# A diffusion trunk on one core: where layer 1's S5 and Hyena preparations stand beside layer 0's context mixer

## The chip, the cores and the metric

The kernel runs on one core of a Trainium2 chip. The time is what the device takes for one execution, in microseconds (us). Engines: PE (TensorE, matrix products; it has two clock levels, 1.2 and 2.4 GHz, and the profile gives the share it was granted), DVE (VectorE), ACT (ScalarE), POOL (GpSimd, which here mainly issues gathers and a few loads), and SP, whose queue issues most DMAs.

## The reference

Two layers work on 512 latent tokens (`x`) and 256 context tokens (`xc`) of width 1024. The context leaves after layer 0.

```python
for layer in range(DEPTH):                       # DEPTH = 2
    h  = modulate(rms_norm(x, norm1_g), sh1, sc1)
    hc = modulate(rms_norm(xc, norm1_g), mc[0], mc[1])
    y, yc = token_mixer(h, hc, ...)              # attention, Hyena, S5, gates, merge
    x = x + g1 * y
    h = modulate(rms_norm(x, norm2_g), sh2, sc2)
    x = x + g2 * peer_ffn(h, wq, keys, u, v)
    if need_ctx:                                 # layer 0
        xc = xc + mc[2] * yc
        hc = modulate(rms_norm(xc, norm2_g), mc[3], mc[4])
        xc = xc + mc[5] * peer_ffn(hc, wq, keys, u, v)

def peer_ffn(x):                                 # per block of 128 tokens
    s = einsum('bthsk,hsnk->bthsn', (x @ wq), sub_keys)    # scores, 8 heads x 2 halves
    s_top, i_top = top_k(s, 16)                            # picks
    best, pos = top_k(all sums of two halves, 16)
    gate = softmax(best)
    act = gelu(x . u[expert]);  return sum(gate * act * v[expert])
```

The Hyena branch needs the spectrum of a filter that depends on the layer's weights alone, and the S5 branch needs tables of powers, also from weights alone. Those two are the preparations of the title.

## The kernel before

One Python program writes all instructions; nothing loops on the chip. `weave` takes several generators, each with a lane and a price per step, and always steps the one whose priced time is least, so it fixes the order in which the engines' queues are filled. Between two steps a generator yields a cost in a planner's unit. A scheduler may still shift single instructions.

After layer 0's latent mixer one `weave` runs five chains:

- the main chain: `ctx_rest`, the context's mixer (norm, queries, attention, `hyena_in`, `hyena_out`, `s5_out`, merge), whose end is marked `c1`; then `ctx_side`, the context's norm, scores and picks for its feed-forward part;
- `peer_u`: 128 u blocks, each a load `w` of 128 experts' rows, a split in two parts (`wh` on ACT, `wl` on DVE), 24 matmuls of 512 columns into `pu`, a gelu `ua`, a store;
- `aside`, the side chain that the change touches;
- `gather`: for the two context blocks, 128 gathers of expert rows `gx` by POOL, each with a product on DVE (L1196), then 128 gathers with a weighted add (L170); `gx` has four buffers. It starts when the context's picks and the `gx` pool are there;
- layer 1's modulation vectors.

A latent block is scored (`scores`, PE), picked (`pick`: top-16 searches on DVE, no PE work), and made into a table (`table`, 32 steps: one `ohB` and four `ohA` operations on DVE, four matmuls, a copy `ge`; every fourth step a store of 1 MB). When the side chain has all four tables and u is done, `peer_v` runs 128 v blocks of 24 matmuls into `pa`, with the rest of the gathers beside it. Then layer 1 begins.

`s5_prep` (L368) is a long chain of small DVE operations, then `X<-cmp,cmq` operations of 128x512, transposes on PE, copies on ACT and stores on SP. `hy_prep` (L610) makes a filter, splits it (`FH`, `FL`), and for each half of the columns multiplies it by four DFT matrices; each is a 1 MB load `dft` that POOL issues (L676), in one buffer for layer 1.

Of the kernel before, what the change touches and what calls it, by code (L numbers as in the profile page):

```python
# [23 lines left out]
TL = 512  # L24
# [22 lines left out]
class Trunk:  # L47
# [52 lines left out]
    def weave(self, *chains):  # L100


        run = [[0.0, i, g, w, lane] for i, (g, w, lane) in enumerate(chains)]
        outer, held = self.lane, []
        while run:
            assert len(held) < len(run), (self.done, [c[1] for c in run])
            c = min(x for x in run if x not in held)
            self.lane = c[4]
            known = len(self.done)
            try:  # L110
                d = next(c[2])
            except StopIteration:
                run.remove(c)
                held = []
                continue
            if d == WAIT:
                held = held * (len(self.done) == known) + [c]
                continue
            for x in held:
                x[0] = max(x[0], c[0])  # L120
            held = []
            c[0] += (2.6 if d is None else d) * (c[3]() if callable(c[3]) else c[3])
        self.lane = outer
# [4 lines left out]
    def until(self, *ks):  # L128
        while any(k not in self.done for k in ks):
            yield WAIT  # L130
# [5 lines left out]
    def part(self, g, k):  # L136

        for d in g:
            if d == k:
                return  # L140
            yield d
# [9 lines left out]
    def mark(self, k):  # L151
        self.done.add(k)
        yield 0.0
# [90 lines left out]
    def rows(self, pool, l, j, i, tag="rowb", bufs=1):  # L244
        b = self.t(pool, [128, D], tag=tag, bufs=bufs)
        self.nc.sync.dma_start(b, self.mod[l][j:j + 1, i * D:(i + 1) * D].to_broadcast([128, D]))
        return b
# [1170 lines left out]
    def run(self):  # L1418
# [21 lines left out]
        def mods(l, groups, *vecs):  # L1440
            for g in groups:
                yield from self.mod_group(l, g)
            for w in vecs:
                vec[l, w] = self.mod_vec(l, 3 * w, w)

        def chain(*gens):
            for g in gens:
                yield from g
# [8 lines left out]
        call, until, mark, weave, part = self.call, self.until, self.mark, self.weave, self.part  # L1457


        x1, x2, c1, c2 = new(xl), new(xl), new(xc), new(xc)  # L1460
# [12 lines left out]
        sc, scC = rows(4), rows(2)  # L1473
        act = [self.d([128, TL]) for _ in range(128)]
        C = {}
        hs = []

        def aside():
            yield from self.norm_to(hs[0], x1, vec[0, 1], 0, True)
            self.done.add("h")  # L1480
            yield from self.s5_prep(1, self.S[1], True)
            yield from self.hy_prep(1, TL, self.K[1, TL], True)
            self.done |= {("hy", 1), ("room", 1)}
            with self.pool("pg", True) as pg, ExitStack() as ex:
                hn, w, dot = ([self.t(pg, [128, n]) for _ in range(2)] for n in (D, 3 * 128, 128))
                ids = [self.t(pg, [128, 128], I32) for _ in range(2)]
                pc = [x.rearrange("p (a h k) -> p a h k", a=3, h=8) for x in w]
                C.update({q: (hn[q], pc[q], ids[q], dot[q]) for q in range(2)})
                self.done.add("pg")
                pk = [self.t(pg, [128, 3, 8, 16]) for _ in range(2)]  # L1490
                yield from self.scores(0, hs[0], sc)
                for q in range(5):
                    if q < 4:
                        yield from self.pick(0, sc[q], pk[q % 2])
                    if q:
                        yield from self.table(pk[(q - 1) % 2], G[q - 1])
                    if q == 4 and "gx" not in C:
                        yield from until("c1")
                    if "c1" in self.done and "gx" not in C:
                        C["gx"] = ex.enter_context(self.pool("gx", True))  # L1500
                        self.done.add("gx")
                self.done.add("tabs")
                yield from self.stop("tables")
                yield from until("c2")

        def ctx_side():
            yield from until("pg")
            hn = [C[q][0] for q in range(2)]
            with self.pool("ph") as ph:
                hA = self.halves(ph, TC)  # L1510
                yield from self.norm_to(hA, c1, vec[0, 1], 1, False, hn)
                self.natural(ph, 0, 1, hn)
                yield from self.peer_scores(0, ph, hA, TC, scC)
            for q in range(2):
                yield from self.pick(0, scC[q], C[q][1], C[q][2], False)
                self.done.add(("ids", q))

        def gather():
# [3 lines left out]
            self.done.add("c2")  # L1522

        side, gather = aside(), gather()
        with self.pool("ha") as ha:
            hs.append(self.halves(ha, TL))
            with self.psum(m=4, u=2, s=2), self.pool("ua") as ua:
                weave((chain(self.ctx_rest(0, xc, c1, vec[0, 0], st[0]), mark("c1"), ctx_side()), lambda: 1.1 if "c1" in self.done else 1.0, "m"),
                      (chain(until("h"), self.peer_u(0, ua, hs[0], TL, lambda i: act[i], "tabs"), mark("u")), lambda: 1.2 if "c1" in self.done else 10.0, "u"),
                      (part(side, "tables"), lambda: 1.25 if "c1" in self.done else 1.23 if "pg" in self.done else 0.8, "s"),  # L1530
                      (self.while_(gather, "tabs"), 1.69, "s"), (mods(1, range(6), 0, 1), 1.26, "m"))
            self.done.add(("mods", 1))
            with self.pool("pv", True) as pv:
                vl = self.peer_v(0, pv, hs[0], lambda i: act[i], G, x1, self.store(x2), 0)
                next(vl)
                with self.psum(a=7, x=1):
                    weave((vl, 1.0, "m"), (gather, 1.5, "s"))
# [12 lines left out]
        act = [self.d([128, 128 * nd]) for _ in range(128)]  # L1550
        sc = rows(4)
# [14 lines left out]
        with self.pool("pg", True) as pg, self.pool("fin") as fin:  # L1566
# [7 lines left out]
            with self.pool("ha") as ha:  # L1574
                h = self.halves(ha, TL)
# [141 lines left out]
```

## Time and profile before

| | |
|---|---|
| median of 3 runs | 5657.81 us (5644.19 to 5683.04) |
| profiled execution | 5662.23 us, span 5660.2 us |
| PE, DVE, ACT, POOL busy | 87%, 66%, 31%, 25% of the span |
| mean granted PE clock | 0.925 |
| DMA | 1333 MB, 236 GB/s on average |

Busy is the time in which an engine has an instruction in work. Ends of matmuls are modelled, and they overlap, so a PE that reads as busy may still have room. The granted clock is a share of 2.4 GHz.

### The profile page before, as it was taken

What the parts mean: (1) busy time and instruction counts of PE and PEld (TensorE: products, weight loads), DVE (VectorE), ACT (ScalarE), POOL (GpSimd) and SP (SyncE); (2) the same over time, 40 slices, a digit from 0 to 9 for tenths busy, and PEclk for the clock granted to TensorE, in tenths of its full rate; (3) what the DMA queues carried; (4) which work ended last, traced back from release to release, by engine and by line L of the source; (5) the groups of instructions that cost most, each with busy time, mean ns of one, the idle gap of its engine ahead of it and who ended that gap; (6) DMA issues with size and microseconds to landing.
All of it is one profiled execution on the core that took longest, in us unless ns stands there. A gap on an engine that the chain in (4) does not pass through costs nothing.

```text
span 5660.2 us, 72445 instructions
## 1 busy us (share of the span) xinstructions
PE 4899.3 (87%) x25801; PEld 4022.5 (71%) x25801; DVE 3729.2 (66%) x7594; ACT 1758.3 (31%) x2651; POOL 1426.1 (25%) x1626
## 2 busy tenths in 40 slices
PE   6798978869997888998888887998889588899898
PEld 5676657648885777786666676875678587798687
DVE  5643436644499899987676775534435989788755
ACT  3222423314432322332222223333233133333233
POOL 0003500000002343433444440405000322254400
PEclk7899989889998999999998998998999899999999
DMA  6557335666556888899999986561545777799975
GB/s 207 190 185 263 106 117 183 201 205 185 176 179 207 306 291 314 319 325 343 319 317 311 320 307 205 166 224 58 157 157 168 242 252 243 256 338 333 333 239 176
DMA packets 641793, 1333.38 MB, mean 236 GB/s; under 512 B 56437, under 2 KB 342390, under 8 KB 626328
## 3 DMA queue, kind: packets, MB, share of 16 engines
q1 hardware_dynamic: 522776, 871.53, 47.1%
q0 software_dynamic: 118656, 457.23, 23.0%
q8 instruction: 203, 3.33, 0.2%
q14 instruction: 158, 1.29, 0.1%
HBM read 1147.01 MB, written 181.49 MB: 235 GB/s over the span
## 4 chain that ended last, share of the span: by engine, by line
PE 27%; DVE 12%; DMA 11%; issue 10%; POOL 4%; ACT 1%; SPq 1%; POOLq 0%; DVEq 0%; ACTq 0%
PE pa L181 9%; PE two L181 4%; PE ps L181 4%; PE pu L181 3%; POOL gx L1183 3%; PE px L181 2%; DMA va<-t 2%; PE pf L181 2%; DMA gx<-in_peer_v_dram,t 2%; DVE t L170 2%; DVE wl L160 2%; PE pm L181 2%; DMA gx<-in_peer_un_dram,t 1%; DVE gx L1196 1%; DMA t<-ge 1%
## 5 line engine op out<-in xcount | busy, mean ns | idle before, releaser
L176 ACT CAST wh<-w 128x1024 fp32r<-128x1024 f32 (+1 forms) x550 | 545.9, 993 | 1611.2 <-PE pu L181 395.3
L160 DVE TENSOR_TENSOR wl<-w,wh 128x1024 fp32r<-128x1024 f32 (+1 forms) x550 | 639.4, 1164 | 555.4 <-ACT wh L176 545.3
L1183 POOL DMA_INDIRECT gx<-in_peer_un_dram,t x384 | 527.9, 1375 | 1501.1 <-DVE t L1196 691.6
L181 PE MATMUL pa<-xl,vwh 128*128 128x512 f32 x1664 | 673.1, 405 | 124.1 <-DVE xl L160 123.7
L1183 POOL DMA_INDIRECT gx<-in_peer_v_dram,t x384 | 543.6, 1416 | 680.1 <-DVE t L170 579.9
L181 PE MATMUL pa<-xh,vwh 128*128 128x512 f32 x1664 | 665.8, 401 | 28.1 <-ACT xh L176 21.4
L181 PE MATMUL pu<-t,wh 128*128 128x512 f32 x2048 | 659.0, 403 | 28.5 <-ACT ua L173 20.7
L181 PE MATMUL pa<-xh,vwl 128*128 128x512 f32 x1664 | 665.1, 400 | 1.2 <-DVE ss L167 1.1
L181 PE MATMUL pm<-t,wh 128*128 128x384 f32 (+1 forms) x2432 | 586.0, 328 | 59.1 <-ACT wh L176 54.4
L170 DVE SCALAR_TENSOR_TENSOR t<-gx,t,t 128x1024 f32<-128x1024 f32 x381 | 488.4, 1282 | 35.2 <-DMA gx<-in_peer_v_dram,t 33.3
L1196 DVE CUSTOM_DVE_ANT_0 gx<-gx,t 128x1024 f32<-128x1024 f32 x384 | 465.3, 1220 | 57.8 <-DMA gx<-in_peer_un_dram,t 57.4
L181 PEld LDWEIGHTS pm<-t,wh 128*128 128x128 f32 x2432 | 431.1, 196 | 77.7 <-ACT wh L176 72.2
L181 PEld LDWEIGHTS pa<-xl,vwh 128*128 128x128 f32 x1664 | 323.0, 194 | 213.2 <-DVE xl L160 147.0
L181 PEld LDWEIGHTS pu<-t,wh 128*128 128x128 f32 x2048 | 389.6, 194 | 111.6 <-ACT ua L173 26.8
L181 PE MATMUL pu<-t,wl 128*128 128x512 f32 x1024 | 412.9, 404 | 60.4 <-DVE wl L160 60.4
L181 PE MATMUL pm<-t,wl 128*128 128x384 f32 (+1 forms) x1216 | 396.9, 329 | 49.1 <-DVE wl L160 49.0
L181 PEld LDWEIGHTS pa<-xh,vwh 128*128 128x128 f32 x1664 | 322.0, 194 | 103.6 <-ACT xh L176 27.7
L176 ACT CAST vwh<-gt 128x512 fp32r<-128x512 f32 (+1 forms) x256 | 145.3, 568 | 794.9 <-PE pa L181 671.2
L181 PEld LDWEIGHTS pa<-xh,vwl 128*128 128x128 f32 x1664 | 323.5, 194 | 70.8 <-DVE vwl L160 3.5
L176 ACT CAST xh<-x 128x1024 fp32r<-128x1024 f32 x256 | 268.2, 1048 | 252.4 <-DMA x<-in_peer_v_dram 208.0
L160 DVE TENSOR_TENSOR xl<-x,xh 128x1024 fp32r<-128x1024 f32 x256 | 312.7, 1221 | 26.2 <-ACT xh L176 25.8
L160 DVE TENSOR_TENSOR gt<-va,gt 128x512 f32<-128x512 f32 (+1 forms) x256 | 156.6, 622 | 262.2 <-DMA va<-t 107.9
(371 smaller groups left out, 9154.3 us busy)
## 6 DMA issues: line engine op xcount, KB each, us to landing
w<-in_peer_u_dram SPq DMA_DIRECT2D x256, 512.0 KB
x<-in_peer_v_dram SPq DMA_DIRECT2D x256, 512.0 KB
w<-in_in_w_dram SPq DMA_DIRECT2D x128, 512.0 KB
t<-ge SPq DMA_DIRECT2D x56, 1024.0 KB
gt<-t SPq DMA_DIRECT2D x112, 512.0 KB
w<-in_mod_w_dram SPq DMA_DIRECT2D x96, 512.0 KB
dft<-in_dft_dram POOLq DMA_DIRECT2D x32, 1024.0 KB, 6.8
t<-ua SPq DMA_DIRECT2D x128, 256.0 KB
```

Source lines behind the costliest of these rows:

```text
L160: return (e or self.nc.vector).tensor_tensor(out=out, in0=a, in1=b, op=op)
L170: self.nc.vector.scalar_tensor_tensor(out=out, in0=a, scalar=s, in1=b, op0=op0, op1=op1)
L176: self.nc.scalar.copy(h, x)
L181: self.nc.tensor.matmul(out, l, r, start=start, stop=stop)
L1183: self.nc.gpsimd.indirect_dma_start(out=g, out_offset=None, in_=src, in_offset=bass.IndirectOffsetOnAxis(ap=ids[:, k:k + 1], axis=0))
L1196: self.nc.vector.tensor_tensor_reduce(out=g, in0=g, in1=x, scale=1.0, scalar=0.0, op0=OP.mult, op1=OP.add, accum_out=dot[:, c:c + 1])
```

## The change

In `aside` the latents' scores move ahead of everything else. The picks and tables follow at once. `s5_prep` and `hy_prep` of layer 1 move into the loop over the blocks, to the point where `c1` is found done (it is waited for at the fourth round now, not at the fifth), after the `gx` pool is taken. The price of a u block ahead of `c1` goes from 10 to 5.

```diff
         def aside():
             yield from self.norm_to(hs[0], x1, vec[0, 1], 0, True)
             self.done.add("h")
-            yield from self.s5_prep(1, self.S[1], True)
-            yield from self.hy_prep(1, TL, self.K[1, TL], True)
-            self.done |= {("hy", 1), ("room", 1)}
+            yield from self.scores(0, hs[0], sc)
             with self.pool("pg", True) as pg, ExitStack() as ex:
...
                 pk = [self.t(pg, [128, 3, 8, 16]) for _ in range(2)]
-                yield from self.scores(0, hs[0], sc)
                 for q in range(5):
                     if q < 4:
                         yield from self.pick(0, sc[q], pk[q % 2])
                     if q:
                         yield from self.table(pk[(q - 1) % 2], G[q - 1])
-                    if q == 4 and "gx" not in C:
+                    if q == 3 and "gx" not in C:
                         yield from until("c1")
                     if "c1" in self.done and "gx" not in C:
                         C["gx"] = ex.enter_context(self.pool("gx", True))
                         self.done.add("gx")
+                        yield from self.s5_prep(1, self.S[1], True)
+                        yield from self.hy_prep(1, TL, self.K[1, TL], True)
+                        self.done |= {("hy", 1), ("room", 1)}
...
-                      (chain(until("h"), self.peer_u(...), mark("u")), lambda: 1.2 if "c1" in self.done else 10.0, "u"),
+                      (chain(until("h"), self.peer_u(...), mark("u")), lambda: 1.2 if "c1" in self.done else 5.0, "u"),
```

DVE's queue in the context's `hyena_out` (`hy`, `hz`, `hyl` are its products and split). Before, S5 operations `cmp`, `cmq`, `X` stand between them:

```order
L160 TENSOR_TENSOR cmp_9615<-X_9414,t_8211 128x512
L160 TENSOR_TENSOR cmq_9616<-X_9414,t_8235 128x512
L160 TENSOR_TENSOR X_9414<-cmp_9615,cmq_9616 128x2x16x16
L160 TENSOR_TENSOR hy_9593<-pm_9569,hk_9567 128x512
L160 TENSOR_TENSOR hz_9594<-pm_9569,hk_9567 128x512
L160 TENSOR_TENSOR hy_9593<-hy_9593 128x256
L160 TENSOR_TENSOR cmp_9669<-X_9414,t_8211 128x512
L160 TENSOR_TENSOR hy_9593<-hz_9594 128x256
L160 TENSOR_TENSOR cmq_9670<-X_9414,t_8235 128x512
```

After, at the same place of the context's mixer, a pick's searches (MAX, MAX_INDEX, MATCH_REPLACE on a block's scores `scin`):

```order
L1053 MAX_INDEX i_2034_9571<-s_2033_9570,scin_9966 128x8
L1054 MATCH_REPLACE mr_10074<-s_2033_9570,scin_9966 128x128
L1055 MAX s_2033_9570<-mr_10074 128x8
L1056 MAX_INDEX i_2034_9571<-s_2033_9570,mr_10074 128x8
L160 TENSOR_TENSOR hy_9880<-pm_9849,hk_9847 128x512
L160 TENSOR_TENSOR hz_9881<-pm_9849,hk_9847 128x512
L160 TENSOR_TENSOR hy_9880<-hy_9880 128x256
L1054 MATCH_REPLACE mr_10080<-s_2033_9570,scin_9966 128x128
L160 TENSOR_TENSOR hy_9880<-hz_9881 128x256
```

So the S5 operations left this place and a pick came.

POOL's queue at layer 1's `hy_prep`. Before, the `dft` loads stand alone or between the merge's small adds `mf`:

```order
L676 DMA dft_10408<-in_dft_dram 128x2048
L676 DMA dft_10650<-in_dft_dram 128x2048
L160 TENSOR_TENSOR mf_10585<-mf_10585,sg_10665 128x256
L676 DMA dft_10788<-in_dft_dram 128x2048
L160 TENSOR_TENSOR mf_10585<-mf_10585,sg_10734 128x256
L676 DMA dft_10928<-in_dft_dram 128x2048
```

After, they stand between the context's gathers:

```order
L1183 DMA gx_17108<-in_peer_un_dram,t_9563 128x1024
L676 DMA dft_16656<-in_dft_dram 128x2048
L1183 DMA gx_17148<-in_peer_un_dram,t_9563 128x1024
L1183 DMA gx_17166<-in_peer_un_dram,t_9563 128x1024
L1183 DMA gx_17215<-in_peer_un_dram,t_9563 128x1024
L676 DMA dft_16729<-in_dft_dram 128x2048
L1183 DMA gx_17221<-in_peer_un_dram,t_9563 128x1024
```

A load and two to five gathers now follow each other in one queue.

DVE's queue at the end of the last table, just ahead of the first v block (`gt`, `xl`). Before, `wl` of the last u blocks stands among the last steps:

```order
L160 TENSOR_TENSOR ohB_21433<-t_82,pt_20379 128x512
L167 TENSOR_SCALAR ohA_21432<-t_82,pt_20379 128x128 x4
L160 TENSOR_TENSOR wl_21514<-w_21512,wh_21513 128x1024
L160 TENSOR_TENSOR wl_21548<-w_21546,wh_21547 128x1024
L160 TENSOR_TENSOR ohB_21449<-t_82,pt_20379 128x512
L167 TENSOR_SCALAR ohA_21448<-t_82,pt_20379 128x128 x4
L160 TENSOR_TENSOR wl_21582<-w_21580,wh_21581 128x1024
L160 TENSOR_TENSOR gt_21620<-va_21634,gt_21620 128x32x16
```

After, steps and gather adds alone:

```order
L160 TENSOR_TENSOR ohB_21638<-t_82,pt_21094 128x512
L170 SCALAR_TENSOR_TENSOR t_9557<-gx_21631,t_9559,t_9557 128x1024
L167 TENSOR_SCALAR ohA_21637<-t_82,pt_21094 128x128 x4
L170 SCALAR_TENSOR_TENSOR t_9557<-gx_21634,t_9559,t_9557 128x1024
L160 TENSOR_TENSOR ohB_21654<-t_82,pt_21094 128x512
L167 TENSOR_SCALAR ohA_21653<-t_82,pt_21094 128x128 x4
L170 SCALAR_TENSOR_TENSOR t_9557<-gx_21650,t_9559,t_9557 128x1024
L170 SCALAR_TENSOR_TENSOR t_9557<-gx_21666,t_9559,t_9557 128x1024
L160 TENSOR_TENSOR gt_21686<-va_21700,gt_21686 128x32x16
```

The last `wl` moved ahead of the whole last table.

## Rows read from the trace of the kernel before

**Rows 1.** The page's span in 40 equal slices: busy tenths of two engines.

```profile
PE   6798978869997888998888887998889588899898
...
DVE  5643436644499899987676775534435989788755
```

**Rows 2.** Windows: busy us (instructions) of each engine, PE clock, DMA share, GB/s.

```profile
core 0: us, PE busy (x) PEld busy (x) DVE busy (x) ACT busy (x) POOL busy (x), PEclk, DMA share, GB/s
956.00:1186.00 230.00, 182.54 (x1168) 136.76 (x1168) 156.22 (x382) 70.63 (x131) 2.17 (x4) 0.82 0.63 202
1186.00:1340.00 154.00, 121.31 (x809) 98.31 (x808) 64.25 (x106) 50.31 (x74) 8.33 (x12) 0.90 0.70 206
1340.00:1517.00 177.00, 177.00 (x1160) 161.56 (x1160) 69.82 (x89) 74.49 (x105) 11.46 (x12) 1.00 0.56 167
1517.00:1789.00 272.00, 232.79 (x1237) 196.54 (x1237) 232.74 (x929) 95.98 (x144) 22.19 (x18) 0.94 0.60 190
1789.00:2522.00 733.00, 658.89 (x3270) 552.12 (x3269) 682.41 (x1604) 222.47 (x328) 299.05 (x217) 0.96 0.86 305
...
2547.00:3404.00 857.00, 733.83 (x3017) 588.35 (x3018) 627.92 (x784) 203.03 (x255) 374.83 (x270) 0.92 0.93 320
```

**Rows 3.** The chain that ended last, 2405 to 2425: start, us, what.

```profile
2412.93 5.46 PE pu L181 x24
```

**Rows 4.** Timeline of DVE, 2457 to 2459.5: start us, us, engine line op.

```profile
2455.89 1.22 DVE L160 TENSOR_TENSOR wl<-w,wh 128x1024 fp32r<-128x1024 f32 x1
2457.03 0.69 DVE L160 TENSOR_TENSOR ohB<-t,pt 128x512 f32<-128x512 f32 x1
2457.63 1.11 DVE L167 TENSOR_SCALAR ohA<-t,pt 128x128 f32<-128x128 f32 x4
2458.66 0.69 DVE L160 TENSOR_TENSOR ohB<-t,pt 128x512 f32<-128x512 f32 x1
```

**Rows 5.** DVE's groups, 1556 to 1789: busy us, mean ns | idle before.

```profile
L160 DVE TENSOR_TENSOR wl<-w,wh 128x1024 fp32r<-128x1024 f32 x39 | 47.3, 1213 | 4.7 <-ACT wh L176 4.7
...
L1196 DVE CUSTOM_DVE_ANT_0 gx<-gx,t 128x1024 f32<-128x1024 f32 x14 | 17.0, 1217 | 4.1 <-DMA gx<-in_peer_un_dram,t 4.1
```

**Rows 6.** DVE's groups, 956 to 1340 (`cmp` and `cmq` cost as `X` does).

```profile
L160 DVE TENSOR_TENSOR X<-cmp,cmq 128x512 f32<-128x512 f32 x32 | 21.9, 686 | 16.6 <-PE ps L181 16.3
...
L160 DVE TENSOR_TENSOR FL<-fst,FH 128x512 fp32r<-128x512 f32 x8 | 5.5, 690 | 1.7 <-ACT FH L176 1.6
...
L160 DVE TENSOR_TENSOR win<-win,ps 128x512 f32<-128x512 f32 x8 | 5.4, 684 | 2.5 <-PE ps L181 1.9 <-DMA win<-in_hy_win_dram 0.6
```

**Rows 7.** Timelines of POOL and PE, 1186 to 1330: in brackets idle before, releaser.

```profile
1229.25 0.53 POOL L676 DMA_DIRECT2D dft<-in_dft_dram  x1 [35.05 <-PE ps L181]
1242.96 0.53 POOL L676 DMA_DIRECT2D dft<-in_dft_dram  x1 [13.18 <-PE ps L181]
1266.78 0.53 POOL L676 DMA_DIRECT2D dft<-in_dft_dram  x1 [23.29 <-PE ps L181]
1276.65 0.53 POOL L676 DMA_DIRECT2D dft<-in_dft_dram  x1 [9.35 <-PE pm L181]
...
1236.67 0.58 PE L181 MATMUL ps<-FH,dft 128*128 128x256 f32 x1 [4.06 <-DMA dft<-in_dft_dram]
...
1258.53 0.58 PE L181 MATMUL ps<-FH,dft 128*128 128x256 f32 x1 [11.39 <-DMA dft<-in_dft_dram]
...
1273.21 0.39 PE L181 MATMUL ps<-FH,dft 128*128 128x256 f32 x1 [1.16 <-DMA dft<-in_dft_dram]
```

**Rows 8.** The chain that ended last, 3430 to 3460: from the v loop into layer 1.

```profile
3434.11 1.29 DVE t L170
3435.41 6.93 DMA gx<-t
...
3445.84 5.97 DMA w<-in_s_w_dram
...
3454.21 1.12 DVE junk L256
```

More of the change, by code (lines that the diff above doesn't have):

```diff
@@ L1528, in run @@
                 weave((chain(self.ctx_rest(0, xc, c1, vec[0, 0], st[0]), mark("c1"), ctx_side()), lambda: 1.1 if "c1" in self.done else 1.0, "m"),
-                      (chain(until("h"), self.peer_u(0, ua, hs[0], TL, lambda i: act[i], "tabs"), mark("u")), lambda: 1.2 if "c1" in self.done else 10.0, "u"),
+                      (chain(until("h"), self.peer_u(0, ua, hs[0], TL, lambda i: act[i], "tabs"), mark("u")), lambda: 1.2 if "c1" in self.done else 5.0, "u"),
                       (part(side, "tables"), lambda: 1.25 if "c1" in self.done else 1.23 if "pg" in self.done else 0.8, "s"),
```

## The prediction

> **What bounds the kernel now.** I read the slices of the span first [rows 1]: VectorE (DVE) is at 9 tenths from about 1,560 us to 2,510 us and at 2 to 6 tenths before that. Then I cut that part of the span into stretches and asked for each engine's busy time and TensorE's (PE's) granted clock in each [rows 2]; the page's 87% for PE mixes stretches with different limits. What the reader is to see there:
>
> - 956 to 1340 (layer 1's S5 preparation, then its Hyena preparation, beside the context's mixer): nobody is full. PE is busy 183 + 121 = 304 of 384 us, at a clock of 0.82 and 0.90, DVE 156 + 64 = 220.
> - 1340 to 1517 (the latents' scores beside the merge): PE is busy for all 177 us, clock 1.00, DVE for 70.
> - 1517 to 1789 (context scores, picks): PE and DVE 233 each, of 272.
> - 1789 to 2522 (tables, gathers, u blocks): DVE 682 of 733, 93%. PE's 659 look alike but are not: a u block of 24 matmuls takes 5.46 us where nothing holds it [rows 3], and the 96 blocks here need 524 us.
>
> So c1, the end of the context's mixer (about 1,517), divides a part that waits from a part that DVE sets.
>
> **What moves, in DVE time.** Costs are from one start to the next, since records overlap a little [rows 4]: a one-hot step of a table is 2458.66 - 2457.03 = 1.63 us, a `wl` 1.14 us, an operation of 128x512 0.60 us. A pick: DVE's 233 us in 1517 to 1789, less 47 of `wl`, 17 of products [rows 5] and some 10 of other things, are 159 for about 3.6 picks, so 44 us each. By the order of the built programs, ahead of c1 now stand the picks of latents 0 and 1 and 14 of the 32 steps of table 0, and 11 u blocks where there were 6.
>
> Out of the part behind c1 go 2 x 44 + 14 x 1.63 + 5 x 1.14 = 117 us of DVE. Into it come the S5 preparation (32 each of `X`, `cmp`, `cmq` at 0.60, 58 us [rows 6], and some 20 of small operations, an estimate), the Hyena preparation (`FL` and `win` 11 us [rows 6], and as much again in small ones, 22) and 20 more gather adds, which the order shows ahead of the last table's end (123, were 103), at about 1.2: 124 us. **DVE, the engine that sets this part, is not relieved: +7 us.** What can be won or lost is how well the waits of either part are covered.
>
> **Ahead of c1.** PE's own work stays: 192 dft matmuls of 256 columns and 192 small ones leave; at half of 5.46/24 = 0.23 us [rows 3] that is 44 us. Five u blocks (27) and the step matmuls (56, some 6) enter: -11. What the stretch 956 to 1340 holds beyond its work is 80 us of idle PE (384 - 304) and what the low clock costs, 183 x 0.18 + 121 x 0.10 = 45. The Hyena preparation's waits for its 1 MB `dft` loads go, and the scores, PE work without chains, move to where attention's chains leave gaps. But the 16 S5 outputs and `hyena_out` now run beside picks, which give PE nothing, and their DVE operations stand in line behind clumps of MAX8 rows. Nearest rows: 1340 to 1517 has no idle PE, 956 to 1186 has 20%. I let about half go, 60 us; with the 11, **-71**. Ends: everything goes, -136; nothing but PE's own work, -10.
>
> **Behind c1.** The Hyena preparation now stands among gathers and u blocks. Its `dft` tile has one buffer: POOL issues a load, it lands, PE does its 24 matmuls, POOL may issue the next. The trace has rounds of 13.7, 23.8 and 9.9 us (issues at 1229.25, 1242.96, 1266.78, the next at 1276.65), with landings of 7.4, 15.6 and 6.4 us until PE starts [rows 7]. Mean 15.8; eight rounds make 126 of the stretch of 154 us, 28 are the rest. I take the same with 6 us for u blocks in the way: 160 us. DVE's work in it by the order: 41 products (1.16), 18 `wl` and the 22 us, 90 us, at 93% 97 us. So some **+63** of the DVE-bound part in which DVE is not full. Ends: rounds of 9.9, +10; rounds of 23.8 (218 us), +121. I keep the mean, since DMA share is 0.63 to 0.70 where these rounds ran and 0.86 where they go.
>
> By the Trainium skill ("DMA: Bandwidth & Descriptors", section "Anatomy of one DMA") a load costs 2.0 us and its bytes over 436 GB/s, an estimate of 4.4 us for 1 MB. The landings in the trace, 6.4 to 15.6 us, say otherwise; by the page's price a round would be some 10 us, the term +11, and the sum some 50 us lower.
>
> POOL's queue: behind each `dft` load that waits for PE stand gathers, whose products DVE must do in order, ahead of the next `wl`. Four `gx` buffers let the gathers run three ahead, about 3 x 3.4 us (733 us for 217 gathers, POOL's count in [rows 2]), so a wait of 10 us is covered; the 13.18 us one is, but for 3. I book nothing more. SP's queue: 32 stores of `X` and the S5 weight stores now stand among u loads; a late `w` load costs up to 5.97 us [rows 8]. This, and the last table, whose 32 steps stand without any u block behind u's end (DVE stays full with steps and adds, PE has almost nothing, and its clock must rise again), I put at **+5**, ends 0 and +20. With DVE's +7: **+75**, from +17 to +148.
>
> **Behind the tables.** In 2547 to 3404 the gathers lack 20 adds, 10.5 MB, 33 us at 320 GB/s if DMA sets that stretch, nothing if not; PE is busy 734 of 857 us and the fixed pattern is its own, so **-5**. At the end, the last add now stands at 3434.11, its residual's load takes 6.93 us, and layer 1's norm only begins at 3454.21 [rows 8]. By the order the gather now ends some ten blocks of the v loop earlier, so this chain goes: **-15**, from -5 to -20.
>
> **Sum.** -71 + 75 - 5 - 15 = -16 us on the profiled execution's 5662 us, 5646. The median of the three runs is 4 us under that execution; I say **5645**.
>
> **Rivals.**
>
> *No change worth measuring (my forecast).* About 1%, 57 us, is what a measurement of this kernel can tell from no change. The stalls move with the preparations. Own range 5600 to 5700.
>
> *Faster: the regimes fill each other.* Picks take DVE where PE was the limit, preparations take PE where DVE is, and the stalls of 956 to 1340 vanish, as in 1340 to 1517, where no PE time is idle. Nearly all of it goes (-130) and the rounds are short (+10, +7, +5 behind c1): with -20 at the end -128, 5535. Half-way cases lie at 5570. For it: 220 of 384 us of DVE busy, room for both picks. Against it: DVE's sum behind c1 does not fall. The Trainium skill ("Perfetto Trace Analysis", section "Optimization Strategy") says that where the most-contended engine changes over time, interleaving the regimes may help; that is this rival, and 1517 to 1789, where both engines hold 86%, agrees with it.
>
> *Slower: POOL's queue closes a loop.* A `dft` load waits for PE; the gathers queued behind land late; DVE stands at their product, with `wl` behind it; PE's u block waits for that `wl`, and the next round's matmuls stand behind the block. Rounds then last as the longest of the trace: +121. With -40 ahead of c1, +7, +10 and -15: +83, 5745. It decides from waits of POOL at `dft` above the 10 us that three gathers cover. For it: two of the three waits shown are longer (13.18, 23.29) [rows 7]. Against: they were long when POOL had nothing else and came early.
>
> **Chances.** Forecast 0.53, faster 0.27, slower 0.20. For over 1% faster I give 0.27, within 1% 0.52, over 1% slower 0.21. The range, 5560 to 5740, leaves out the full gain and the far end of the loop.
>
> **What would show it.** The end of the context's mixer (last context `my` on DVE) at about 1,445 instead of 1,517, with PE's clock above 0.9 in between; DVE busy below 70% for some 150 us while `ps<-FH,dft` matmuls run beside gathers; the first `pa` matmul within 30 us of 2,547; a stretch of some 100 us before it with PE under a third busy; and no residual load between the last v block and layer 1. I am wrong if the context's mixer ends before 1,400 or after 1,500, if `dft` rounds are 10 or 24 us, or if the v loop's 857 us move by more than 20.

## The result, and the profile after

The changed kernel takes 5715.05 us (median of 5 runs, 5712.15 to 5720.62), the kernel before 5656.69 us in the same session. The ratio is 1.0099, with a 95% interval from 1.0075 to 1.0122: about 56 us slower, right at the 57 us that the prediction took as the least that can be told from no change. The forecast was 5645. The time lies inside the range given, but the change went the other way.

The slices of the span of the changed kernel:

```profile
PE   6898878978997889886888888999789688899898
...
DVE  5643435366778679997676775444345889788755
```

Against [rows 1], VectorE's row of nines behind the context's mixer is broken up: sixes and sevens stand there now. Windows of the kernel before, the parts ahead of and behind c1 and two stretches of the second (the columns are those of [rows 2]):

```profile
929.00:1525.00 596.00, 504.12 (x3289) 410.59 (x3290) 307.61 (x615) 215.59 (x339) 21.96 (x28) 0.89 0.63 196
1525.00:2547.00 1022.00, 905.10 (x4547) 758.81 (x4545) 912.63 (x2529) 319.74 (x475) 321.24 (x235) 0.95 0.79 274
1525.00:1585.00 60.00, 52.77 (x303) 45.29 (x302) 32.44 (x105) 28.43 (x49) 0.00 (x0) 0.94 0.60 190
1585.00:1725.00 140.00, 133.10 (x721) 112.37 (x720) 139.02 (x624) 54.97 (x79) 0.00 (x0) 1.00 0.54 166
```

The same of the changed kernel: both parts first, then stretches of them in order of time, and all that follows the tables:

```profile
933.00:1501.00 568.00, 491.45 (x3223) 398.70 (x3224) 329.18 (x883) 229.51 (x348) 16.69 (x20) 0.93 0.60 186
1501.00:2628.00 1127.00, 960.06 (x4612) 796.93 (x4610) 918.57 (x2284) 318.94 (x474) 347.48 (x264) 0.89 0.79 269
...
1218.00:1392.00 174.00, 128.09 (x813) 99.63 (x813) 123.42 (x403) 56.40 (x79) 6.39 (x6) 0.87 0.55 158
...
1521.00:1601.00 80.00, 80.00 (x524) 71.06 (x524) 44.77 (x81) 37.15 (x66) 0.00 (x0) 1.00 0.61 194
...
1599.00:1730.00 131.00, 126.80 (x651) 107.22 (x650) 111.01 (x424) 42.27 (x63) 5.19 (x4) 0.93 0.52 167
1730.00:1878.00 148.00, 110.88 (x433) 86.56 (x432) 130.86 (x359) 29.96 (x40) 41.91 (x34) 0.83 0.73 237
...
1951.00:2067.00 116.00, 98.90 (x464) 84.35 (x463) 55.63 (x89) 24.99 (x37) 35.77 (x34) 0.87 0.85 289
...
2507.00:2607.00 100.00, 61.90 (x267) 54.29 (x267) 94.75 (x196) 18.06 (x32) 40.96 (x36) 0.60 0.81 275
...
2628.00:5717.00 3089.00, 2704.29 (x13431) 2266.97 (x13431) 2055.03 (x3637) 942.13 (x1370) 894.01 (x919) 0.94 0.73 246
```

What the reader is to see. Ahead of c1 the kernel is 28 us shorter (596 to 568), behind c1 105 us longer (1022 to 1127), and from the first v block on 24 us shorter (5660 - 2547 = 3113 to 3089). The sum, +53, and a start that is 4 us later make the 57 us between the two spans. Behind c1 VectorE does the same work in both, 913 and 919 us; it is idle for 208 us where it was idle for 109. That is the loss. The view of waits says for what VectorE waits there, first in the kernel before (us in total, times, longest):

```profile
DVE wl L160 <- ACT wh L176: 24.0, 10, 4.4
```

and in the changed kernel:

```profile
DVE wl L160 <- ACT wh L176: 95.0, 24, 11.0
DVE gt L160 <- DMA va<-t: 18.4, 1, 18.4
...
DVE t L160 <- DMA wse<-t: 6.6, 1, 6.6
DVE X L160 <- PE ps L181: 6.3, 1, 6.3
DVE wse L360 <- DMA t<-wse: 5.9, 1, 5.9
```

The first row leads through ACT to PE: ACT's `wh` of a u block waits for the matmuls of an earlier one to free its buffer (315 us of ACT's waits in this part; 384 before, but then VectorE had picks to do meanwhile). So VectorE has done all that its queue holds ahead of a `wl` and stands at it, while PE is behind with the u blocks. The second row (`gt`) is no difference: the first v block's `gt` waits for 19.0 us in the kernel before as well, but starts just behind the window's end at 2547, so that the view leaves it out. Three places hold most of it. At 1521 to 1601 the context's scores, u blocks and the second half of the first table stand together; all three need PE, which has no idle time at full clock, and VectorE works for 45 of 80 us. At 1599 to 1878, in the S5 preparation, 37 us are idle. At 1878 to 2067, in the Hyena preparation, 83 are; the row from 1951 shows its dft matmuls, PE at 99 and VectorE at 56 of 116 us. In the kernel before, VectorE is idle for 28 us at 1525 to 1585, most of them beside the end of the latents' scores and the context's norm. Nearly all of the context's scores (key products from 1564 to 1662) and u blocks then stood beside picks: 140 us in which both engines are full.

### The profile page after: what moved, and what is told of

It reads as the page before. It is cut to its first block, busy times and chain, and to the rows that moved or that the text cites. A ratio compares the mean times of both kernels' runs of the same rounds, so it can differ in the third digit from the quotient of the medians.

```text
span 5717.6 us, 72447 instructions
## 1 busy us (share of the span) xinstructions
PE 4935.1 (86%) x25801; PEld 4048.4 (71%) x25801; DVE 3730.8 (65%) x7594; ACT 1771.0 (31%) x2659; POOL 1422.0 (25%) x1626
## 4 chain that ended last, share of the span: by engine, by line
PE 34%; DVE 18%; DMA 15%; issue 9%; POOL 4%; ACT 2%; SPq 1%; DVEq 0%; POOLq 0%; ACTq 0%
PE pa L181 9%; PE ps L181 6%; PE pm L181 6%; PE two L181 4%; PE pu L181 3%; DMA va<-t 3%; POOL gx L1183 3%; DVE wl L160 2%; DMA gt<-t 2%; DVE t L170 2%; PE px L181 2%; PE pf L181 2%; DVE gx L1196 2%; DMA t<-ge 2%; DMA gx<-in_peer_v_dram,t 1%
## 5 line engine op out<-in xcount | busy, mean ns | idle before, releaser
L181 PE MATMUL pu<-t,wh 128*128 128x512 f32 x2048 | 671.6, 408 | 27.8 <-ACT ua L173 24.7
L181 PE MATMUL ps<-ohB,ohA 128*128 128x128 f32 x1792 | 275.1, 307 | 76.0 <-DVE ohA L167 38.8
```

The source lines that it names most:

```text
L181: self.nc.tensor.matmul(out, l, r, start=start, stop=stop)
```

## The experiments

Differences to the kernel before are given as ratios with their 95% intervals, and as us by the ratio and 5655 us. My first theory, A, was that the preparations bring chains and waits into the part behind c1, and the rival, B, that something else does, the last table without u blocks above all; C, D and E came up on the way and are stated in the texts on record.

**One part undone at a time.** Layer 1's S5 preparation back ahead of the scores:

```diff
+            yield from self.s5_prep(1, self.S[1], True)
             yield from self.scores(0, hs[0], sc)
...
-                        yield from self.s5_prep(1, self.S[1], True)
```

> The changed kernel with layer 1's S5 preparation back ahead of the latents' scores; the Hyena preparation stays behind c1. Theory A (the loss sits behind c1, where the preparations put chains and waits into the part that VectorE sets): 58 us of VectorE's work and some 40 us of its waits leave that part, some 60 us come back ahead of c1: 5,670 to 5,690 us. Theory B (the loss is the last table without u blocks, because u ends early; the preparations cost the same at either place): 5,700 to 5,730 us.

Measured: 5699.03 us, ratio 1.0073 (1.0049 to 1.0097), +41. The Hyena preparation back:

```diff
+            yield from self.hy_prep(1, TL, self.K[1, TL], True)
             yield from self.scores(0, hs[0], sc)
...
-                        yield from self.hy_prep(1, TL, self.K[1, TL], True)
```

> The changed kernel with layer 1's Hyena preparation back ahead of the latents' scores; the S5 preparation stays behind c1. Theory A: the 154 us stretch behind c1 in which VectorE was busy for 94 goes, with it some 60 us of waits and 22 us of work, and some 50 us come ahead of c1: 5,675 to 5,695 us. Theory B: 5,700 to 5,730 us.

Measured: 5700.82, 1.0079 (1.0052 to 1.0107), +45. The u price back:

```diff
-lambda: 1.2 if "c1" in self.done else 5.0, "u"),
+lambda: 1.2 if "c1" in self.done else 10.0, "u"),
```

> The changed kernel with the u blocks' price ahead of c1 at 10, as before: by the order of the program 6 u blocks ahead of c1 instead of 11, and u ends 5 blocks later, still ahead of the last table's end. Theory A: PE's 27 us move from ahead of c1, where PE is near full, to behind it, where it has room: 5,690 to 5,715 us. Theory B: the stretch of the last table without u blocks shortens by half: 5,680 to 5,700 us. If the u blocks ahead of c1 fill gaps there: 5,715 to 5,730 us.

Measured: 5708.05, 1.0093 (1.0064 to 1.0121), +53. And the tail without u blocks taken away:

```diff
-lambda: 1.2 if "c1" in self.done else 5.0, "u"),
+lambda: 1.35 if "c1" in self.done else 5.0, "u"),
```

> The changed kernel with the u blocks' price behind c1 at 1.35 instead of 1.2, so that u ends with the last table and fewer u blocks stand in each stretch before. Theory A: the tail's waits (20 us) go, but VectorE, which sets the part, has the same work: 5,690 to 5,710 us. Theory B: the tail was the loss: 5,660 to 5,690 us.

Measured: 5721.74, 1.0127 (1.0093 to 1.0160), +72. So B falls: the last table without u blocks is not the loss, a slower u gains nothing. A is right on the place and wrong on the sizes: undoing a part gives back 15, 11 or 3 of 56 us, each within what the intervals leave open. Windows of the kernel with the S5 preparation back, both parts and a stretch of its context scores:

```profile
927.00:1525.00 598.00, 519.72 (x3305) 419.84 (x3298) 345.88 (x897) 228.00 (x349) 21.40 (x20) 0.92 0.60 189
1525.00:2576.00 1051.00, 915.73 (x4527) 759.95 (x4525) 855.44 (x2233) 319.11 (x474) 297.04 (x230) 0.93 0.76 264
1584.00:1664.00 80.00, 80.00 (x502) 69.92 (x502) 25.61 (x28) 32.15 (x52) 0.00 (x0) 1.00 0.57 177
```

The part behind c1 is 76 us shorter than in the changed kernel, the part ahead 30 longer, and all behind the tables 36 longer (3125 to 3089). The last goes with fewer gather adds done by then, as shown below. VectorE is idle for 196 us behind c1, with 64 us less work there: the context's scores now leave it idle for 54 of 80 us.

**The u price alone, in the kernel before.**

```diff
-lambda: 1.2 if "c1" in self.done else 10.0, "u"),
+lambda: 1.2 if "c1" in self.done else 5.0, "u"),
```

> The kernel before with the u blocks' price ahead of c1 at 5, the one part of the change that moves no preparation; 11 u blocks ahead of c1 instead of 6. If the parts add up (29 us more ahead of c1 and 12 us less behind, from the run with price 10 in the changed kernel): 5,665 to 5,675 us, with c1 some 25 us later than before. If u blocks fill gaps beside the preparations: 5,640 to 5,655 us.

Measured over ten runs: 5674.31, 1.0035 (1.0019 to 1.0051), +20; ahead of c1 617 us, behind it 1024. The parts added up as expected: 5 u blocks cost 21 us ahead and save nothing behind. In the other direction, 1 u block ahead of c1:

```diff
-lambda: 1.2 if "c1" in self.done else 10.0, "u"),
+lambda: 1.17 if "c1" in self.done else 55.0, "u"),
```

> The kernel before with the u blocks' price ahead of c1 at 55 and behind it at 1.17: 1 u block ahead of c1 instead of 6, and u ends with the last table as before. If u blocks cost ahead of c1 what price 5 cost (20 us for 5 blocks more): 5,630 to 5,640 us, with c1 some 25 us earlier. If 5 blocks fewer only lengthen the part behind: 5,650 to 5,665 us.

Measured: 5688.62, 1.0065 (1.0048 to 1.0082), +37: ahead 585, behind 1062. So it missed; 5 blocks fewer ahead save 11 us there and cost 40 behind. Price 10 stands at a good place between the two.

**What the preparations cost where they stand.** Both left out of the changed kernel:

```diff
-                        yield from self.s5_prep(1, self.S[1], True)
-                        yield from self.hy_prep(1, TL, self.K[1, TL], True)
+                        self.S[1] = self.S[0]
+                        self.K[1, TL] = self.K[0, TL]
```

> The changed kernel without layer 1's S5 and Hyena preparations (layer 1 reads layer 0's tables and filter spectrum instead, so its values differ and its work does not). The time gives the price of both where they stand: 5,715 less this in the changed kernel, 5,653 less this in the kernel before. Theory A (behind c1 the preparations cost VectorE's work of them, 81 us, and the waits of their chains on top): 5,530 to 5,570 us, so 145 to 185 us after and 85 to 125 us before. Theory B (their place costs nothing, something else of the change does): 5,620 to 5,660 us.

Measured: 5562.64, 0.9835 (0.9810 to 0.9861), -93. By the ratios the two cost 149 us in the changed kernel. The 93 us below the kernel before are not their price there, since this kernel keeps the rest of the change, the u price above all; the kernel before without both was not run. The S5 preparation left out of the changed kernel (the first of these lines):

> The changed kernel without layer 1's S5 preparation (layer 1 reads layer 0's tables). If it costs behind c1 what VectorE does in it (about 79 us) and some 30 us of idle VectorE beside it: 5,600 to 5,615 us. If its waits are covered: 5,630 to 5,645 us.

Measured: 5611.81, 0.9931 (0.9912 to 0.9950), -39: it costs 95 us behind c1. And out of the kernel before, in the same way:

> The kernel before without layer 1's S5 preparation; picks then come ahead of c1 sooner. If ahead of c1 it stands in time that the context's mixer leaves free, and its place is what the change pays for: 5,600 to 5,630 us, that is 25 to 55 us for it, half or less of its price in the changed kernel. If its price is the same at both places: 5,545 to 5,575 us.

Measured: 5603.01, 0.9918 (0.9898 to 0.9938), -46: it costs 46 us ahead of c1. Without it the changed kernel and the kernel before are within 7 us of each other. (In these three kernels the tables end sooner, so some u blocks move into the v loop, and the times alone are comparable, not the parts.)

**Where the Hyena preparation's idle time comes from.** Two dft buffers instead of one:

```diff
-                    c = self.dft(pool, T, fc, nt, 2 if l == 0 else 1)
+                    c = self.dft(pool, T, fc, nt, 2)
```

> The changed kernel with two dft buffers instead of one in layer 1's Hyena preparation, so that a load can land while PE works on the one before. If the rounds load, land, multiply are what that preparation costs behind c1 (the prediction's +63): 5,660 to 5,685 us, with VectorE above 80% where the dft matmuls run. If the cost is in the chain of the filter ahead of them and in VectorE's own work: 5,700 to 5,720 us.

Measured: 5710.48, 1.0096 (1.0072 to 1.0120), +54. One load for all rounds:

```diff
                 for fc in range(nt):
-                    c = self.dft(pool, T, fc, nt, 2 if l == 0 else 1)
+                    if l == 0 or hf == fc == 0:
+                        c = self.dft(pool, T, fc, nt, 2 if l == 0 else 1)
```

> The changed kernel with one dft load for all eight rounds of layer 1's Hyena preparation instead of one each (so that its spectrum is wrong; its matmuls and all other work stay). Theory A, in the prediction's form (a round is load, landing, multiply, and this is what leaves VectorE idle there): 5,655 to 5,685 us, VectorE above 80% beside the dft matmuls. Theory C (PE, with the dft matmuls and a u block in each round, fills the round, and loads are hidden or nearly): 5,695 to 5,715 us, as with two buffers.

Measured: 5701.36, 1.0085 (1.0056 to 1.0114), +48. Windows of the two, the stretch of their dft matmuls, first with two buffers:

```profile
1945.00:2040.00 95.00, 80.73 (x418) 67.72 (x419) 50.00 (x80) 21.87 (x32) 28.16 (x28) 0.91 0.82 296
```

then with one load:

```profile
1954.00:2040.00 86.00, 79.76 (x422) 67.88 (x421) 48.64 (x79) 21.99 (x33) 26.70 (x22) 0.96 0.78 260
```

The stretch falls from 116 to 95 and 86 us, and the whole part behind c1 by 20 in both. VectorE is still at 53% and 57% there. VectorE's idle time in the stretch falls from 60 us to 45 and 37, so loads make up 15 to 23 of the 60. The rest fits theory C: PE does some 11 u blocks beside the eight rounds (256 matmuls `pu` in those 116 us) and is busy for 93% of the stretch without loads, while VectorE waits at `wl` (36 of the 60 us). In the whole time the 20 us show as 2 and 8, less than the intervals.

**Picks ahead of c1, with both preparations there.** In the kernel before:

```diff
-lambda: 1.2 if "c1" in self.done else 10.0, "u"),
+lambda: 1.08 if "c1" in self.done else 10.0, "u"),
-lambda: 1.25 if "c1" in self.done else 1.23 if "pg" in self.done else 0.8, "s"),
+lambda: 1.25 if "c1" in self.done else 0.9 if "pg" in self.done else 0.6, "s"),
```

> The kernel before with the side chain's price ahead of c1 at 0.6 and 0.9 instead of 0.8 and 1.23, and the u blocks' behind c1 at 1.08 instead of 1.2 so that u ends with the tables. Both preparations stay ahead of c1, and 15 of 32 steps of picks that stood behind it join them. Theory A (VectorE's work sets the part behind c1, and the part ahead has VectorE idle for a third of its time): behind c1 40 to 60 us less, ahead 10 to 40 more: 5,620 to 5,650 us. Theory B: within 15 us of the kernel before.

Measured: 5721.90, 1.0113 (1.0086 to 1.0139), +64. Ahead 668, behind 944: 78 us less behind c1, more than A has, but 72 more ahead, which it has not; 8 u blocks and 39 more gather adds were left for the v loop, and all behind the tables took 62 us longer (3113 to 3175). VectorE was idle for 288 of 596 us ahead of c1 in the kernel before, and this idle time was not free room. But the 72 us are not the picks' price alone. The picks wait for the latents' scores, and the kernel before has 85 of their 384 matmuls of 512 columns and 32 of their 128 key products behind c1; here all of them stand ahead of it, some 20 us of PE at 0.23 us a matmul. VectorE's work there grew by 37 us.

**Open points.** Does the gathers' late end, by itself, cost the boundary's time? In the kernel before:

```diff
-                    weave((vl, 1.0, "m"), (gather, 1.5, "s"))
+                    weave((vl, 1.0, "m"), (gather, 1.3, "s"))
```

> The kernel before with the gathers' price beside the v blocks at 1.3 instead of 1.5, and nothing else: by the order of the program the context's feed-forward part ends some 13 v blocks before the v loop does, as it does in the changed kernel. If the late end of the gathers sets the start of layer 1 (the prediction's boundary term): 5,630 to 5,640 us, with no residual load between the v loop and layer 1's norm. If the extra gathers only delay v blocks: 5,650 to 5,665 us.

Measured over twelve runs: 5668.29, 1.0013 (1.0001 to 1.0025), +7. No gain: no residual's load stands between the last v block and layer 1's norm any more, but the loop with its denser gathers takes 817 us to its last `gt` product where it took 804. The same line with the S5 preparation back (the first experiment's edit):

> The changed kernel with layer 1's S5 preparation back ahead of the scores and the gathers' price beside the v blocks at 1.3. With the S5 preparation back alone, the two parts around c1 became 45 us shorter in the profile, but the time fell by 16 only, and the last gather add came 26 us behind layer 1's norm. If that late end took the rest: 5,665 to 5,680 us. If the S5 preparation's place is worth no more than 16 us: 5,695 to 5,705 us.

Measured: 5700.93, 1.0070 (1.0047 to 1.0093), +40. As without it; so the S5 preparation's place is worth some 15 us once the rest is changed. What counts behind the tables is how many gather adds are left. VectorE's groups behind c1, in the changed kernel:

```profile
L170 DVE SCALAR_TENSOR_TENSOR t<-gx,t,t 128x1024 f32<-128x1024 f32 x124 | 158.7, 1279 | 15.3 <-DMA gx<-in_peer_v_dram,t 15.0
```

and in the one with the S5 preparation back:

```profile
L170 DVE SCALAR_TENSOR_TENSOR t<-gx,t,t 128x1024 f32<-128x1024 f32 x89 | 114.0, 1280 | 8.9 <-DMA gx<-in_peer_v_dram,t 8.5
```

35 adds fewer, and 36 us more behind the tables (3125 to 3089). The relation is loose: the six kernels with 124 adds in this part took 3087 to 3108 us behind the tables.

Do the picks hold the context's S5 outputs? In the changed kernel:

```diff
+                yield from until("c1")
                 for q in range(5):
```

> The changed kernel with the latents' picks waiting for c1 as well, so that only the scores and u blocks stand beside the context's mixer. It will be slower (all tables come later). What counts is c1: if picks stand in the way of the mixer's S5 outputs on VectorE, c1 comes 30 to 50 us earlier than in the changed kernel (520 to 535 us behind the start instead of 567); if they use time that is free, at most 15 us earlier.

Measured: c1 555 us behind the start, 12 earlier (one run, 5873.39 us in all). It tells half of what it was meant to: the scheduler still shifted the first pick's searches ahead of c1, where they stand at 1180 to 1250 in its trace. One pick and 14 steps are worth 12 us there. PE's idle time ahead of the context's S5 outputs did not fall: 29.3 us, against 28.0 in the changed kernel. What the first pick is worth stays open.

The Hyena preparation alone moved: the edits of the S5 preparation back, u price 10 and gather price 1.3 together.

> The kernel before with only the Hyena preparation moved behind c1 (scores ahead of picks, S5 preparation first, u price 10), and the gathers' price beside the v blocks at 1.3. If parts add up (the Hyena move some 5 to 15 us longer, the boundary 20 us shorter): 5,635 to 5,655 us. If the Hyena preparation behind c1 costs its idle VectorE, some 60 us: 5,680 to 5,700 us.

Measured: 5695.11, 1.0061 (1.0040 to 1.0083), +34. The gathers' price alone had measured +7. Ahead 576, behind 1071; VectorE's work behind c1 is 42 us less than before (871 to 913) and its idle time 91 more (200 to 109).

Two orders, to find what the parts share. The first table moved behind both preparations:

```diff
-                for q in range(5):
...
+                for q in range(2):
+                    yield from self.pick(0, sc[q], pk[q])
+                yield from until("c1")
+                yield from self.s5_prep(1, self.S[1], True)
+                C["gx"] = ex.enter_context(self.pool("gx", True))
+                self.done.add("gx")
+                yield from self.hy_prep(1, TL, self.K[1, TL], True)
...
+                for q in range(4):
+                    yield from self.table(pk[q % 2], G[q])
+                    if q < 2:
+                        yield from self.pick(0, sc[q + 2], pk[q % 2])
...
-lambda: 1.2 if "c1" in self.done else 5.0, "u"),
+lambda: 1.38 if "c1" in self.done else 5.0, "u"),
```

> The changed kernel with the first table moved behind both preparations, so that at c1 the S5 preparation (VectorE) stands beside the context's scores (PE) and the Hyena preparation (PE) beside the context's picks (VectorE); the u blocks' price behind c1 is 1.38, so that u nearly reaches the last table's end (that price alone, at 1.35, gave +6 us). Theory D (the change stands like beside like: context scores beside a table and u, dft matmuls beside u, S5 products beside picks; each of the two engines waits in turn): 5,655 to 5,685 us, VectorE idle for under 170 us behind c1 instead of 208. Theory E (idle time behind c1 comes with having the preparations there at all, whatever stands beside them): 5,705 to 5,730 us.

Measured: 5736.76, 1.0158 (1.0129 to 1.0186), +89. A window of it, where the S5 preparation stands beside the context's scores:

```profile
1549.00:1609.00 60.00, 58.03 (x396) 52.01 (x395) 17.71 (x16) 23.82 (x41) 0.00 (x0) 1.00 0.64 200
```

VectorE works for 18 of 60 us although S5's work is there to do: 39 of the 42 idle us are waits at `wl`. Behind c1 it is idle for 205 us in all. The two preparations in the other order:

```diff
-                        yield from self.s5_prep(1, self.S[1], True)
                         yield from self.hy_prep(1, TL, self.K[1, TL], True)
+                        yield from self.s5_prep(1, self.S[1], True)
```

> The changed kernel with the two preparations in the other order: the Hyena preparation beside the context's picks and first products, the S5 preparation behind it. Theory D: 5,680 to 5,700 us, VectorE idle for 20 to 40 us less behind c1. Theory E: 5,705 to 5,725 us.

Measured: 5710.18, 1.0089 (1.0054 to 1.0124), +50, idle for 199. Theory D falls: what stands beside what, in the two orders tried, doesn't change the idle time.

## Why the prediction was wrong, point by point

**VectorE's work behind c1 (+7): right.** It went from 912.6 to 918.6 us.

**Ahead of c1 (-71): mis-sized, -28 measured.** Two steps failed. The first was "I let about half go, 60 us". Idle PE fell from 92 us (596 - 504) to 77 (568 - 491), the loss to the low clock from 504 x 0.11 = 55 to 491 x 0.07 = 34: 36 us, not 60. The second is a term that the sum puts at nothing. PE's own work, busy time by clock, rose from 449 to 457 instead of falling by 11, because not all of the latents' scores stood ahead of c1 in the kernel before. Their matmuls of 512 columns there:

```profile
L181 PE MATMUL ps<-t,wh 128*128 128x512 f32 x200 | 61.9, 391 | 0.0
...
L181 PE MATMUL ps<-t,wl 128*128 128x512 f32 x99 | 38.5, 389 | 0.0
```

and in the changed kernel:

```profile
L181 PE MATMUL ps<-t,wh 128*128 128x512 f32 x256 | 82.5, 404 | 4.1 <-ACT wh L176 4.1
...
L181 PE MATMUL ps<-t,wl 128*128 128x512 f32 x128 | 50.9, 398 | 0.0
```

The other 85 of 384, and 32 of 128 key products, ran behind c1 before, until 1561. At the prediction's 0.23 us a matmul the 85 are 19 us, an estimate; the own work is off by as much. (The 14 table steps are also 112 matmuls in the trace, where the sum has 56.)

The window 1218 to 1392 shows where waits stay: 46 us of idle PE at a clock of 0.87. PE's waits there, with the context's S5 outputs beside picks:

```profile
PE pm L181 <- DMA t<-t: 27.9, 4, 14.9
PE pm L585 <- ACT y L173: 5.3, 3, 1.9
```

PE's waits ahead of c1 in the kernel before:

```profile
PE ps L181 <- DMA dft<-in_dft_dram: 21.7, 6, 11.4
PE pm L181 <- DVE cmq L160: 17.4, 2, 14.6
...
PE pm L181 <- DMA t<-t: 4.0, 4, 2.1
```

The waits for `dft` went, as forecast. The wait of 14.9 us is not new. It stands ahead of the context's first S5 output, and in the kernel before PE waits there for 14.6 us, put down to `cmq`, an operation of the S5 preparation on VectorE. With the u price alone changed, no pick stands ahead of c1, and the same wait is 15.0 us and put down to the load. In all PE's idle time ahead of these outputs is 18.6 us before, 28.0 after, and 28.4 with the u price alone; with the Hyena preparation back it is 0.2. So picks are not what brings it; what does, the runs leave open. The load that PE waits for brings layer 0's S5 tables, stored at 165 to 206 us. The 5 u blocks were priced rightly (27; 31 by the run with price 10, 537 to 568 us).

**Behind c1 (+75): mis-sized, +105 measured.** Idle VectorE grew by 99 us where 68 were booked. The Hyena preparation was booked at +63 and left 83 us idle. (Its ends, +10 and +121, leave out the 6 us for u blocks that the mean has: +16 and +127.) Its rounds were as forecast, 14.9 us in the mean: six from the issue at 1963.50 to that at 2052.58. But what fills them was not: by the two runs with fewer waits for loads the step "a round is load, landing, multiply" holds for 15 to 23 of the 60 idle us beside the dft matmuls; the rest fits PE with the u blocks. The S5 preparation's waits were not booked at all, and its stretch has 37 us of idle VectorE: 13 at `wl`, and two waits for a DMA at the tile `wse` (6.6 for a copy into it, 5.9 for a store that must free it). And nothing was booked for the context's scores, which lost the picks beside them: 35 us of idle VectorE in 80.

**The rival "POOL's queue closes a loop": near in time, not the mechanism.** Gathers behind `dft` loads waited for 0.6 us in all in the changed kernel. Without the loads the time fell by 8 us, less than the intervals tell from nothing.

**The v loop and the boundary (-20): right in sum, -24 measured.** From the first v block the loop took 806 us against 804 to its last `gt` product. The chain of [rows 8] is gone: the last add comes at 3456, ahead of the last v block. But this is not what pays: taken away alone it gave nothing. The gain more likely lies in the 22 adds that were already done (124 against 102 by the groups); that is argued from counts, not shown.

**The rival "the regimes fill each other": fell.** Picks did come where PE was the limit and preparations where VectorE was, and behind c1 both engines idle more: PE 167 us instead of 117, VectorE 208 instead of 109. The rule of the Trainium skill ("Perfetto Trace Analysis", section "Optimization Strategy") that interleaving may help where the most-contended engine changes over time is not borne out by this trace.

**The last table without u blocks (within +5): right.** VectorE was full there, 95 of 100 us, PE at 62 with a clock of 0.60; filling it with u blocks gained nothing.

**The signs.** The context's mixer ended at 1500 instead of 1445, on the bound that the prediction set for being wrong, the first `pa` came 82 us after 2547 instead of within 30, and PE was busy for 62 of the 100 us before it, not under a third. VectorE below 70% beside the dft matmuls (106 of 189 us), rounds near 15 us, the v loop's length and no residual load before layer 1 came as forecast.

**What is shown and what stays open.** Shown: the loss is idle VectorE behind c1; the u price is worth 20 us alone. The S5 preparation costs 95 us behind c1 in the changed kernel and 46 ahead of c1 in the kernel before, but the difference is not the price of its place. Put back ahead of c1 it gives a kernel at +41, where the changed kernel without it is at -39: beside the picks, all of the scores and 11 u blocks it costs 80 us ahead of c1 too. Its place is worth some 15 of the 95. Not explained: the parts don't add. The u price alone costs 20 us, the Hyena preparation alone 34 (with the gathers' price at 1.3), these two together 41, S5 and u 45, S5 and Hyena 53, all three 56; the S5 preparation alone was not moved. Idle VectorE behind c1 is 102 to 141 us in the complete kernels that keep both preparations ahead of c1 and 188 to 211 in those that move one or both (the run with waiting picks aside), however they are ordered. Why the first to move brings nearly all of it, no run here tells. One rival was left untested: the price per step of the side chain behind c1, which sets how many `wl` stand between a preparation's operations, was 1.25 in all runs (only the u blocks' price was varied, to 1.35, with 206 us idle).

## What to carry to other kernels

A balance of the busiest engine's work says little where a second engine is 89% busy in the same part: here VectorE's work stayed and its idle time doubled. Idle time that a profile shows beside a piece of work need not leave with it; look at who waits there, and for whom, before booking it as a gain. Before summing what a move takes along, count on both sides what else changes place with it: here a fifth of the latents' scores did. And where several changes act on one part of a program, measure each alone and in pairs; here the sum of single costs told little of the whole.

## What the runs showed that I had not expected

Idle VectorE ahead of c1 (288 of 596 us) was not free room: 15 pick steps put there, and the last fifth of the latents' scores with them, made that part 72 us longer. One wait can stand under two names: PE's 15 us ahead of the first S5 output are put down to an S5 operation in one trace and to a load in another, and what looked like a new wait was an old one. And fewer gather adds ahead of the v loop showed as about 1 us each behind it (35 adds, 36 us), within some 20 us from kernel to kernel.
